# A two-layer decoder trunk on one core: one block of value products per group, two queues for the first loads, an earlier first norm

## The chip, the cores and the metric

The kernel runs on one core of one Trainium2 chip. The metric is the device time of one execution in microseconds (us); less is better. Five engines share the work: TensorE (PE in the profile, its weight loads are PEld), VectorE (DVE), ScalarE (ACT), GpSimd (POOL) and SyncE (SP), which here only issues transfers. Transfers are issued on the queues of SP, ACT and POOL and are carried by 16 DMA engines.

## The reference

Two pre-norm layers on x of 256 tokens by 2048 features, all float32, and a last norm. Layer 0 mixes by forgetting attention (32 heads of 64), layer 1 by sliding-window attention (32 query heads, 4 key and value heads, a learned sink per head, rotation of 16 of 64 dimensions).

```python
# layer 0
h = rmsnorm(x, norm_g[0]);  p = h @ fox_w_in          # q, k, v, gate: 2048 columns each, and 32 for f
log_f = log_sigmoid(p_f + b_f);  c = cumsum(log_f)
s = q k^T / 8 + c[t] - c[s], causal
y = softmax(s) @ v;  x = x + (y * silu(gate)) @ fox_w_out
# layer 1
h = rmsnorm(x, norm_g[1]);  p = h @ swa_w_in          # q, gate: 2048 columns each, k, v: 256 each
s = rope(q) rope(k)^T / 8, keys of the last 128 tokens
y = softmax with the sink in its sum @ v;  x = x + (y * silu(gate)) @ swa_w_out
# end
rmsnorm(x, final_g)
```

## The kernel before

**Weights as units and parts.** Every projection is cut into units of 256 output columns (`Unit`, L162). A unit is loaded in transfers of up to 1 MB on SP's queue (`load`, L187), split on chip into a rounded high half (a cast on ACT, L203) and a low rest (a subtraction on DVE, L204), and multiplied part by part (`block`, L206): for each of the 16 slices of 128 features a 512-column matmul (high weights on both halves of the activations) and a 256-column one. A part has 1 to 4 slices. A unit makes two accumulators (c = 0 and 1). The order on TensorE is: part i for c = 0, then part i-1 for c = 1. The very first value unit, 288 columns wide with the 32 columns of f, uses three 288-column matmuls per slice.

**Ticks.** Two slices of 512-column matmuls, or two of 256, make one tick (`tick`, L105), so a part of 4 slices is 4 ticks for each c. All attention work is hung into this stream by numbers: `after(n, fn)` (L102) lets `fn` write its instructions n ticks later. A scheduler then places what was written; TensorE's matmuls stay in the order written, other engines' instructions may move ahead where nothing holds them.

**Groups.** Layer 0 has 8 groups of 4 heads (two pairs each), and a group's units are q, k, gate, v. Layer 1 has k and v once, and then 8 groups of q, gate. For each pair (`Pair`, L341): `s` makes scores, softmax and the normalised weights `st`; `t` turns `st` of one head by three transposes into PSUM (`pt`, pool `ps_t`, one buffer) and copies it to `pts`; `pv` multiplies `pts` by the values into PSUM (`psy`, pool `ps_y`, one buffer), multiplies by the gate and splits the result into `ys`. `FOX_DUE`, `FOX_FIRST`, `FOX_LAST`, `SWA_DUE` and `SWA_LAST` (L39 to L43) give the ticks of s, t and pv for the two pairs of a group, counted from the end of that group's k (layer 0) or q (layer 1) for c = 0.

**The start.** Group 0's v, q and k are loaded in small parts (`V_PARTS`, `QK_PARTS`) between slices of x (`XP`, `XF`, L763). `split_x` makes the high and low half of a slice of x, `square_x` sums its squares. `NORM0` = 82 ticks after the start `norm0` (L784) sums the squares over features on TensorE (`ps_n`) and makes the factor r of the first norm. Until r is there, the first group's q, k and v are copied out of PSUM, and what needs r waits in a list (`when_normed`, L422). `FORGET` ticks after the values are scaled, `forget` (L391) transposes the f columns (`zt` into `pt_z`) and makes c; `FORGOT` = 20 ticks later c is transposed back (`pt_c`). The bias of a pair (`bc`) is read back from DRAM by GpSimd, which adds the causal mask `fmask` (L496). 9 matmuls on ones come first (`warm`, L117). The sinks of layer 1 are read at the start on GpSimd's queue (L839).

## Time and profile before

| | us |
|---|---|
| median of 3 runs | 858.47 (857.77 to 859.59) |
| profiled execution, its own time | 857.08 |
| span of that execution in the trace | 855.2 |
| TensorE busy in the span | 837.9 |
| VectorE busy | 665.6 |
| ScalarE busy | 547.9 |
| GpSimd busy | 88.1 |

The mean granted TensorE clock of the core is 0.992 of full speed. The profile's views used below are: the page's busy times and its chain of work that ended last; the waits (who waited for whom); the timeline (one row per run of like instructions: start in us, us to the end of the last, engine, line, operation, operands, count, and in brackets the idle time of the engine before and what ended it); the chain in order of time (start, us, what, count); and windows (for each stretch in us: its length, busy us and count for each engine, granted clock of TensorE, mean busy share of the DMA engines, GB/s).

### The profile page before, as it was taken

What the parts mean: (1) busy time and instruction counts of PE and PEld (TensorE: products, weight loads), DVE (VectorE), ACT (ScalarE), POOL (GpSimd) and SP (SyncE); (2) the same over time, 40 slices, a digit from 0 to 9 for tenths busy, and PEclk for the clock granted to TensorE, in tenths of its full rate; (3) what the DMA queues carried; (4) which work ended last, traced back from release to release, by engine and by line L of the source; (5) the groups of instructions that cost most, each with busy time, mean ns of one, the idle gap of its engine ahead of it and who ended that gap; (6) DMA issues with size and microseconds to landing.
All of it is one profiled execution on the core that took longest, in us unless ns stands there. A gap on an engine that the chain in (4) does not pass through costs nothing.

```text
span 855.2 us, 13619 instructions
## 1 busy us (share of the span) xinstructions
PE 837.9 (98%) x5038; PEld 726.0 (85%) x5038; DVE 665.6 (78%) x1410; ACT 547.9 (64%) x1080; POOL 88.1 (10%) x78
## 2 busy tenths in 40 slices
PE   8989999999999999999999999999999999999995
PEld 6968888888888888888888888888888888888885
DVE  6699968869686886868667778798898889976554
ACT  7576766747566674756655556577676776676562
POOL 1014100202011030300011110000000000003210
PEclk9989999999999999999999999999999999999998
DMA  7856455555555555554375555453544444355523
GB/s 241 282 175 229 167 176 187 191 190 187 184 181 173 190 189 188 191 177 144 128 254 186 176 185 193 155 189 108 190 149 148 148 149 156 140 178 180 191 99 98
DMA packets 28689, 150.51 MB, mean 176 GB/s; under 512 B 3232, under 2 KB 8256, under 8 KB 13008
## 3 DMA queue, kind: packets, MB, share of 16 engines
q1 hardware_dynamic: 25040, 142.09, 47.8%
q0 software_dynamic: 1408, 6.36, 2.5%
q10 hardware_dynamic: 2176, 1.20, 0.5%
q8 instruction: 39, 0.64, 0.3%
q14 instruction: 26, 0.21, 0.1%
HBM read 147.50 MB, written 2.15 MB: 175 GB/s over the span
## 4 chain that ended last, share of the span: by engine, by line
PE 90%; DVE 4%; DMA 3%; ACT 2%; issue 0%; SPq 0%; DVEq 0%; ACTq 0%
PE acc L73 81%; PE ps_s L73 3%; DMA wraw<-in_fox_in_dram 3%; PE psy L73 3%; PE pt L76 2%; DVE w L204 2%; ACT w L203 1%; ACT st L305 0%; DVE st L295 0%; SPq L198 0%; DVE xT L662 0%; DVE gt L276 0%; DVE kk L458 0%; DVE kk L457 0%; ACT xs L155 0%
## 5 line engine op out<-in xcount | busy, mean ns | idle before, releaser
L73 PE MATMUL acc<-xs,w 128*128 128x512 f32 (+1 forms) x2624 | 490.1, 341 | 1.7 <-ACT w L203 1.5
L73 PEld LDWEIGHTS acc<-xs,w 128*128 128x128 f32 x2624 | 408.0, 189 | 62.1 <-issue 4.8
L204 DVE TENSOR_TENSOR w<-wraw,w 128x1024 fp32r<-128x1024 f32 (+3 forms) x271 | 329.5, 1221 | 110.6 <-ACT w L203 108.6
L203 ACT CAST w<-wraw 128x1024 fp32r<-128x1024 f32 (+3 forms) x271 | 277.6, 1028 | 139.9 <-PE acc L73 124.1
L73 PE MATMUL acc<-ys,w 128*128 128x512 f32 x960 | 171.0, 338 | 0.0
L73 PEld LDWEIGHTS acc<-ys,w 128*128 128x128 f32 x960 | 147.5, 189 | 21.5 <-issue 0.5
L73 PE MATMUL acc<-w,xs 128*128 128x256 f32 (+2 forms) x608 | 114.0, 335 | 1.3 <-ACT w L203 0.8
L73 PEld LDWEIGHTS acc<-w,xs 128*128 128x128 f32 x608 | 92.3, 189 | 11.7 <-ACT w L203 1.1
L250 ACT COPY half<-acc 128x256 f32<-128x256 f32 x112 | 41.4, 370 | 46.2 <-PE acc L73 46.0
L305 ACT ACTIVATE st<-st,mx 128x128 f32<-128x128 f32 (+1 forms) x128 | 56.7, 444 | 8.8 <-DVE mx L508 8.1
L496 POOL TENSOR_TENSOR bc<-bc,fmask 128x768 f32<-128x768 f32 x16 | 42.6, 2664 | 49.7 <-DMA bc<-negc_d 46.7
L360 ACT COPY pts<-pt 128x384 f32<-128x384 f32 x64 | 30.4, 475 | 17.6 <-PE pt L76 17.6
L571 POOL TENSOR_TENSOR acc<-acc,sq 128x256 f32<-128x256 f32 x28 | 30.0, 1070 | 105.1 <-ACT sq L565 105.1
L569 POOL COPY acc<-sq 128x256 f32<-128x256 f32 x2 | 1.9, 936 | 337.1 <-ACT sq L565 337.1
L73 PE MATMUL ps_s<-kk,q 128*128 128x128 f32 (+1 forms) x256 | 35.5, 281 | 0.1
L316 DVE TENSOR_SCALAR st<-st,rl 128x128 f32<-128x128 f32 (+1 forms) x128 | 32.4, 316 | 0.8
L73 PEld LDWEIGHTS ps_s<-kk,q 128*128 128x128 f32 x256 | 32.2, 191 | 0.7 <-DVE kk L458 0.2
L76 PE MATMUL pt<-ident,st 128*128 128x128 f32 x192 | 31.8, 274 | 0.6 <-ACT pts L360 0.3
L495 POOL DMA_DIRECT2D bc<-negc_d x16 | 8.7, 547 | 205.5 <-DVE mx L507 146.5
L76 PEld LDWEIGHTS pt<-ident,st 128*128 128x128 f32 x192 | 23.5, 140 | 5.6 <-ACT pts L360 1.4
L156 DVE SCALAR_TENSOR_TENSOR xs<-xT,g_sb,xs 128x256 fp32r<-128x256 f32 x32 | 22.2, 716 | 2.9 <-ACT xs L155 2.9
L305 ACT ACTIVATION_READ_ACCUMULATOR st<-st,mx 128x1 f32 x128 | 23.9, 187 | 0.0
(136 smaller groups left out, 587.7 us busy)
## 6 DMA issues: line engine op xcount, KB each, us to landing
wraw<-in_fox_in_dram SPq DMA_DIRECT2D x58, 1024.0 KB, 4.9
wraw<-in_swa_in_dram SPq DMA_DIRECT2D x36, 1024.0 KB, 4.9
wraw<-in_fox_out_dram SPq DMA_DIRECT2D x14, 1024.0 KB, 4.8
wraw<-in_swa_out_dram SPq DMA_DIRECT2D x14, 1024.0 KB, 4.9
bc<-negc_d POOLq DMA_DIRECT2D x16, 384.0 KB, 3.8
wraw<-in_fox_in_dram SPq DMA_DIRECT2D x6, 512.0 KB, 5.6
wraw<-in_fox_out_dram SPq DMA_DIRECT2D x4, 512.0 KB, 3.6
wraw<-in_swa_out_dram SPq DMA_DIRECT2D x4, 512.0 KB, 3.5
```

The source lines that it names most:

```text
L73: tc.keep_in_program_order(nc.tensor.matmul(*args, **kw))
L76: tc.keep_in_program_order(nc.tensor.transpose(out, in_, ident))
L156: nc.vector.scalar_tensor_tensor(out=xs[:, kt, 1, :], in0=xT[:, kt, :], scalar=g, in1=xs[:, kt, 0, :].bitcast(F32), op0=ALU.mult, op1=ALU. ...
L203: state["split"] = nc.scalar.copy(w[:, :, 0, :], raw)
L204: nc.vector.tensor_tensor(out=w[:, :, 1, :], in0=raw, in1=w[:, :, 0, :].bitcast(F32), op=ALU.subtract)
L250: nc.scalar.copy(s, ps[:, S : 2 * S])
L305: nc.scalar.activation(st[:, hh, rng], st[:, hh, rng], AF.Exp, bias=nm[:, qb, hh : hh + 1], accum_out=l[:, qb, hh : hh + 1],)
L316: nc.vector.tensor_scalar_mul(st[:, hh, rng], st[:, hh, rng], rl[:, qb, hh : hh + 1])
L360: nc.scalar.copy(self.pts[hh], pt[:, 0 : 3 * P])
L495: nc.gpsimd.dma_start(out=bc, in_=negc_d[h0 : h0 + 2, :].partition_broadcast(P))
L496: nc.gpsimd.tensor_add(bc, bc, fmask.unsqueeze(1).to_broadcast([P, 2, 3 * P]))
L571: nc.gpsimd.tensor_add(sums[0], sums[0], s)
```

## The change

- **Value products.** `pv` of each pair is replaced by `Group.values`: both pairs of a group are multiplied in one block into one PSUM tile of 512 columns, at one due time per group. In layer 1, where both pairs of a group use the same values, one product covers both pairs (512 columns and 2x128 instead of twice 256 and 128). The gate product and the split into `ys` run on 512 columns at a time, in place in `gt`; for the last group of layer 1 (`singly`) they run pair by pair. `pts` of a group is one tile per head of the pair.
- **PSUM.** `ps_y` is gone; `ps_t` has two buffers, which transposes and `psy` share.
- **Start.** The first parts of v and q are read on ACT's queue, x entirely on SP's. x comes in 6 transfers of 1, 1, 2, 4, 4, 4 slices instead of 9, and v's last four parts in 2 transfers of 6 slices instead of 4 of 3. `PLAN` writes the order of loads, splits and squares out. 8 warm matmuls instead of 9.
- **First norm.** At tick 62 instead of 82, ahead of the end of the first units, so `when_normed` goes: v's results are scaled as they leave PSUM. `FORGET` is 8.
- **Due times** of the second pair's scores and transposes in layer 0 move by a few ticks.
- **Mask and sinks.** The causal mask is set into `bc` by two selects on its two diagonal blocks instead of an addition of `fmask`. The read of the sinks is written at step 300.

```diff
-WARM = 9
-V_PARTS = (1, 1, 2, 3, 3, 3, 3)
+WARM = 8
+V_PARTS = (1, 1, 2, (3, 3), (3, 3))
-NORM0 = 82
-FORGET = 6
+NORM0 = 62
+FORGET = 8
+SINK = 300
-FOX_DUE = ((16, 34, 80), (32, 58, 106))
-FOX_FIRST = ((46, 66, 90), (62, 82, 106))
-FOX_LAST = ((14, 32, 80), (34, 72, 86))
-SWA_DUE = ((16, 40, 52), (44, 64, 74))
-SWA_LAST = ((26, 45, 56), (30, 56, 68))
+FOX_DUE = ((16, 34), (40, 60), 106)
+FOX_FIRST = ((46, 68), (74, 94), 114)
+FOX_LAST = ((14, 32), (38, 72), 86)
+SWA_DUE = ((16, 40), (44, 64), 74)
+SWA_LAST = ((26, 45), (30, 56), 68)
...
-    ps_t = ctx.enter_context(tc.tile_pool(name="ps_t", bufs=1, space=bass.MemoryType.PSUM))
-    ps_y = ctx.enter_context(tc.tile_pool(name="ps_y", bufs=1, space=bass.MemoryType.PSUM))
+    ps_t = ctx.enter_context(tc.tile_pool(name="ps_t", bufs=2, space=bass.MemoryType.PSUM))
...
-    nc.scalar.dma_start(out=xT[:, 1:2, :], in_=xt_d[:, 1:2, :])
+    raw_v0 = work.tile([P, 6 * P], F32, tag="pts0", name="wraw", bufs=1)
+    nc.scalar.dma_start(out=raw_v0[:, 0 : 256 + H], in_=vf_d[:, 0, :])
+    raw_q0 = work.tile([P, S], F32, tag="row", name="wraw", bufs=4)
+    nc.scalar.dma_start(out=raw_q0, in_=fox_in_d[0, 0, 0][:, 0, :])
...
-        def pv(self):
-            psy = ps_y.tile([P, 512], F32, tag="Y", name="psy")
-            for hh in range(2):
-                o = psy[hh * HD : (hh + 1) * HD, :]
-                mm(o[:, 0:S], self.v_of(0, hh), self.pts[hh][:, 0:S], start=True, stop=False)
-                mm(o[:, P:S], self.v_of(1, hh), self.pts[hh][:, S : 3 * P], start=False, stop=True)
-            yt = work.tile([P, S], F32, tag="row", name="yt", bufs=4)
-            nc.vector.tensor_mul(yt, psy[:, 0:S], self.gate())
-            nc.scalar.copy(ys[:, self.kt, 0, :], yt)
-            nc.vector.tensor_sub(ys[:, self.kt, 1, :], yt, ys[:, self.kt, 0, :].bitcast(F32))
...
+        def values(self, kt, singly, shared):
+            psy = ps_t.tile([P, 512], F32, tag="T", name="psy")
+            for js in [slice(0, 2)] if shared else [slice(j, j + 1) for j in range(2)]:
+                for hh in range(2):
+                    o = psy[hh * HD : (hh + 1) * HD, :].rearrange("p (j n) -> p j n", j=2)[:, js, :]
+                    p = self.pts[hh][:, js, :]
+                    v = [self.v_of(js.start, b, hh) for b in range(2)]
+                    mm(o, v[0], p[:, :, 0:S], start=True, stop=False)
+                    mm(o[:, :, P:S], v[1], p[:, :, S : 3 * P], start=False, stop=True)
+            y = self.gt
+            for js in [slice(j, j + 1) for j in range(2)] if singly else [slice(0, 2)]:
+                out = ys[:, kt + js.start : kt + js.stop]
+                psj = psy.rearrange("p (j n) -> p j n", j=2)[:, js, :]
+                nc.vector.tensor_mul(y[:, js, :], psj, y[:, js, :])
+                nc.scalar.copy(out[:, :, 0, :], y[:, js, :])
+                nc.vector.tensor_sub(out[:, :, 1, :], y[:, js, :], out[:, :, 0, :].bitcast(F32))
...
-            nc.scalar.copy(vg, ps[:, 0:256])
-            nc.scalar.copy(zt, ps[:, 256 : 256 + H])
-            def rest():
-                r = r0()[:, S + c : S + c + 1]
-                nc.scalar.mul(zt, zt, r)
-                nc.scalar.mul(vg, vg, r)
-                if c == 1:
-                    after(FORGET, lambda: forget(state["zt"]))
-            when_normed(rest)
+            r = r0()[:, S + c : S + c + 1]
+            nc.scalar.mul(zt, ps[:, 256 : 256 + H], r)
+            nc.scalar.mul(vg, ps[:, 0:256], r)
+            if c == 1:
+                after(FORGET, lambda: forget(state["zt"]))
...
-                nc.gpsimd.tensor_add(bc, bc, fmask.unsqueeze(1).to_broadcast([P, 2, 3 * P]))
+                for hh in range(2):
+                    diagonal = bc[:, hh, :].rearrange("p (b k) -> p b k", k=P)[:, 0:3:2, :]
+                    fill_where_not(diagonal, [[0, 2], [-1, P]], 0, 1)
...
-    XP = [(0,), (1,), (2, 3), (4, 5), (6, 7), (8, 9), (10, 11), (12, 13), (14, 15)]
-    XF = [3, 6, 9, 9, 12, 13, 15, 16, 19]
+    XP = [(0, 1), (1, 2), (2, 4), (4, 8), (8, 12), (12, 16)]
+    PLAN = "x0 s0 w2 w3 x1 s1 w6 x2 s2 w9 x3 w10 s3 w11 q0 q1 x4 w12 x5 w13 q2 q3 s4 w14 q4 q5 s5 q6 q7 w15 w16"
...
-    nc.gpsimd.dma_start(out=sink, in_=sink_d.partition_broadcast(P))
+    after(SINK, lambda: nc.gpsimd.dma_start(out=sink, in_=sink_d.partition_broadcast(P)))
```

The program's rows at the places that the prediction speaks of follow. `acc` are the accumulators of the units, `xs` the split x, `w` a split part; 128x288 rows belong to the first value unit, 128x512 and 128x256 rows to q, k and, behind `pt_z`, the gate.

TensorE around the first norm, before:

```order
L73 MATMUL acc<-w,xs 128x288 x3
L73 MATMUL ps_n_504<-ssq_109,ones 128x256
L73 MATMUL ps_n_504<-ones,ssq_109 128x1 x2
L73 MATMUL acc<-w,xs 128x288 x6
L73 MATMUL acc<-xs,w 128x512 x4
L73 MATMUL acc<-xs,w 128x256 x4
L73 MATMUL acc<-xs,w 128x512 x4
L76 MATMUL pt_z<-ident,zt 32x128 x2
```

TensorE around the first norm, now (two more rows, of 4 matmuls with 512 and 4 with 256 columns, and then `pt_z` follow on the last row shown):

```order
L73 MATMUL ps_n_419<-ssq_108,ones 128x256
L73 MATMUL ps_n_419<-ones,ssq_108 128x1 x2
L73 MATMUL acc<-xs,w 128x256 x4
L73 MATMUL acc<-w,xs 128x288 x9
L73 MATMUL acc<-xs,w 128x512 x4
L73 MATMUL acc<-xs,w 128x256 x4
L73 MATMUL acc<-w,xs 128x288 x18
L73 MATMUL acc<-xs,w 128x512 x4
L73 MATMUL acc<-xs,w 128x256 x4
L73 MATMUL acc<-w,xs 128x288 x9
L73 MATMUL acc<-xs,w 128x512 x4
L73 MATMUL acc<-xs,w 128x256 x4
```

Between `ps_n` and `pt_z` TensorE had 18 matmuls; now it has 72. Ahead of `ps_n` stood 50 accumulating matmuls more than now, and `pt_z` stands 4 further back. ScalarE at the same place now (the casts of `w` with a DMA wait are those of the next parts to come, the one behind the two `r_n` rows is the gate's first):

```order
L210 CAST w<-wraw 128x4x256 [waits DMAHW7_49,DVE_49,PE_49]
L147 ACTIVATE r_n_425<-v_n_423 128x258 [waits DVE_49]
L148 ACTIVATE r_n_425<-r_n_425 128x258 [waits Activation_49]
L210 CAST w<-wraw 128x4x256 [waits DMAHW0_49,PE_49]
L482 ACTIVATE zt<-acc,r_n_425 128x32 [waits DVE_49,PE_49]
L483 ACTIVATE vg<-acc,r_n_425 128x256
L210 CAST w<-wraw 128x4x256 [waits PE_49]
L257 COPY half<-acc 128x256 [waits PE_49]
L482 ACTIVATE zt<-acc,r_n_425 128x32 [waits PE_49]
```

The scaled f columns (`zt`), which `pt_z` waits for, are now read from PSUM in one step each, and stand behind the casts of the gate's first two parts.

GpSimd at the start, before:

```order
L113 DMA bf_sb<-in_bf_dram 32x1
L389 MEMSET once 32x256
masks.py:197 MEMSET ident 128x128
L832 MEMSET fmask 128x384
masks.py:199 ISA
masks.py:199 AFFINE_SELECT ident<-ident 128x128 [waits Pool_49]
L122 AFFINE_SELECT fmask<-fmask 128x128 [waits Pool_49]
L122 AFFINE_SELECT fmask<-fmask 128x128
L839 DMA sink<-in_sink_dram 128x32
L836 COPY smask<-fmask 128x384 [waits Pool_49]
L122 AFFINE_SELECT smask<-smask 128x128 [waits Pool_49]
L404 DMA negc_d<-once 32x128 [waits DVE_49]
```

and now:

```order
L116 DMA bf_sb<-in_bf_dram 32x1
L407 MEMSET once 32x256
masks.py:197 MEMSET ident 128x128
L834 MEMSET smask 128x384
masks.py:199 ISA
masks.py:199 AFFINE_SELECT ident<-ident 128x128 [waits Pool_49]
L125 AFFINE_SELECT smask<-smask 128x128 [waits Pool_49]
L125 AFFINE_SELECT smask<-smask 128x128 x2
L839 DMA sink<-in_sink_dram 128x32
L422 DMA negc_d<-once 32x128 [waits DVE_49]
```

The read of the sinks, though written at step 300, stands where it stood: one select further back, ahead of the first row that waits for the forget gate, and with no wait of its own.

TensorE at the value products of layer 1, before (the four `psy` rows come twice per group) and now (once per group):

```order
L73 MATMUL acc<-xs,w 128x256 x4
L73 MATMUL psy<-pts,vs 64x256
L73 MATMUL psy<-pts,vs 64x128
L73 MATMUL psy<-pts,vs 64x256 [waits Activation_49]
L73 MATMUL psy<-pts,vs 64x128
L73 MATMUL acc<-xs,w 128x512 x4
```

```order
L73 MATMUL acc<-xs,w 128x512 x4
L73 MATMUL psy<-pts,vs 64x512 [waits Activation_49]
L73 MATMUL psy<-pts,vs 64x2x128
L73 MATMUL psy<-pts,vs 64x512 [waits Activation_49]
L73 MATMUL psy<-pts,vs 64x2x128
L73 MATMUL acc<-xs,w 128x256 x4
```

Eight products in two places have become four in one. In layer 0 the eight products stay eight, in one place.

More of the change, by code (lines that the diff above doesn't have):

```diff
@@ L190, in load @@
         if off == 0:
-            for tag, size, bufs in STAGES:
-                if unit.early and total * n <= size:
-                    raw = work.tile([P, size], F32, tag=tag, name="wraw", bufs=bufs)
-                    break
+            given = unit.stages[p] if p < len(unit.stages) else None
+            if given is None:
+                raw = wpool.tile([P, 2048], F32, tag="wraw", name="wraw", bufs=3)
+            elif isinstance(given, tuple):
+                tag, size, bufs = given
+                raw = work.tile([P, size], F32, tag=tag, name="wraw", bufs=bufs)
             else:
-                raw = wpool.tile([P, 2048], F32, tag="wraw", name="wraw", bufs=3)
+                raw = given
             raw = raw[:, 0 : total * n].rearrange("p (k n) -> p k n", n=n)
-            nc.sync.dma_start(out=raw, in_=src)
+            if given is None or isinstance(given, tuple):
+                nc.sync.dma_start(out=raw, in_=src)
             unit.raw = raw
@@ L202, in load @@
         w = w[:, 0 : 2 * s * n].rearrange("p (k h n) -> p k h n", h=2, n=n)
-        state["split"] = nc.scalar.copy(w[:, :, 0, :], raw)
+        nc.scalar.copy(w[:, :, 0, :], raw)
         nc.vector.tensor_tensor(
@@ L278, in consume @@
                 silu(group.gt[:, c : c + 1, :])
-                group.gates[c] = g
             elif c == 1:
                 silu(group.gt)
-                group.gates = [group.gt[:, j, :] for j in range(2)]
         return consume
@@ L341, in trunk, with __init__ @@
     class Pair:
-        def __init__(self, kt, scores, v_of, gate, prepare=None):
-            self.kt, self.scores, self.v_of, self.gate = kt, scores, v_of, gate
-            self.prepare = prepare
-            self.pts = [None, None]
+        def __init__(self, j, scores, prepare=None):
+            self.j, self.scores, self.prepare = j, scores, prepare
         def early(self):
@@ L376, in later, with attend @@
             after(s, self.s)
-            after(t, lambda: self.t(0))
-            after(t + 4, lambda: self.t(1))
-            after(pv, self.pv)
+            after(t, lambda: self.t(0, group))
+            after(t + 4, lambda: self.t(1, group))
+    class Group:
+        def attend(self, kt, due, singly, shared):
+            self.pts = [None, None]
+            for j, (s, t) in enumerate(due[0:2]):
+                self.pair(j).later(self, s, t)
+            after(due[2], lambda: self.values(kt, singly, shared))
+        def values(self, kt, singly, shared):
[14 more added lines that the diff above has]
+                nc.vector.tensor_sub(out[:, :, 1, :], y[:, js, :], out[:, :, 0, :].bitcast(F32))
     fox_scope = tc.tile_pool(name="fox", bufs=2)
@@ L460, in k_rest @@
             if c == 0:
-                p0, p1 = self.pair(0), self.pair(1)
-                for pair, d in zip((p0, p1), {0: FOX_FIRST, 7: FOX_LAST}.get(self.g, FOX_DUE)):
-                    pair.later(*d)
+                due = {0: FOX_FIRST, 7: FOX_LAST}.get(self.g, FOX_DUE)
+                self.attend(2 * self.g, due, False, False)
         def v(self, c, ps):
@@ L526, in trunk @@
         if g == 0:
[L527 removed]
+            row, gt, st = ("row", S, 4), ("gt", 2 * S, 3), ("st", 6 * P, 2)
+            uv = Unit(
+                cut(lambda a, b: vf_d[:, a:b], V_PARTS), "tok", G.v, n=256 + H, halves=False,
+                stages=(raw_v0, ("pts1", 6 * P, 1), st),
+            )
             uq, uk = (
@@ L530, in trunk @@
                     cut(lambda a, b, w=fox_in_d[i, 0]: w[a // 8][:, a % 8 : a % 8 + b - a], QK_PARTS),
-                    "wgt", consume, early=True, acc=acc,
+                    "wgt", consume, stages=(first, row, gt), acc=acc,
                 )
-                for i, consume, acc in ((0, G.q, None), (1, G.k, (ps_s, "S")))
+                for i, consume, first, acc in ((0, G.q, raw_q0, None), (1, G.k, row, (ps_s, "S")))
             )
@@ L722, in q @@
             if c == 0:
-                p0, p1 = self.pair(0), self.pair(1)
-                for pair, d in zip((p0, p1), SWA_LAST if self.u == 7 else SWA_DUE):
-                    pair.later(*d)
+                self.attend(2 * self.u, SWA_LAST if self.u == 7 else SWA_DUE, self.u == 7, True)
         def pair(self, j):
```

92 lines of the change are left out of this document (38 added, 54 removed).

## The prediction, made before the changed kernel ran

> **What bounds the kernel now.** I read the page's busy times and chain first, then windows over the whole span, then TensorE's waits, and then the stretch that these point to.
>
> ```profile
> PE 837.9 (98%) x5038; PEld 726.0 (85%) x5038; DVE 665.6 (78%) x1410; ACT 547.9 (64%) x1080; POOL 88.1 (10%) x78
> PE 90%; DVE 4%; DMA 3%; ACT 2%; issue 0%; SPq 0%; DVEq 0%; ACTq 0%
> ```
>
> TensorE is 90% of the chain that ended last. So time goes only by fewer or cheaper matmuls, or where TensorE stands still. Windows (length, busy, clock, DMA share, GB/s) show where that is:
>
> ```profile
> 40.00:45.00 5.00, 4.19 (x26) 3.44 (x24) 2.95 (x4) 2.57 (x5) 0.00 (x0) 1.00 0.84 336
> 45.00:50.00 5.00, 2.19 (x8) 1.82 (x9) 3.96 (x10) 3.93 (x12) 0.00 (x0) 0.66 0.62 218
> 100.00:500.00 400.00, 399.92 (x2382) 345.76 (x2381) 302.47 (x575) 252.09 (x475) 48.90 (x35) 1.00 0.53 184
> 500.00:800.00 300.00, 300.00 (x1834) 259.77 (x1833) 251.89 (x622) 202.33 (x427) 11.53 (x10) 1.00 0.47 162
> ```
>
> From 100 to 800 us TensorE never stops. Between 45 and 50 us it works for 2.19 us only, and its granted clock falls to 0.66. What it waited for (total, times, longest):
>
> ```profile
> PE pt_z L76 <- ACT zt L481: 3.5, 1, 3.5
> PE acc L73 <- ACT w L203: 2.3, 2, 1.5
> PE acc L73 <- DVE w L204: 0.7, 2, 0.4
> PE pt L76 <- ACT pts L360: 0.3, 1, 0.3
> ```
>
> Three sums can thus change: that one wait, the 3.0 us of first loads and splits, and the cost of matmuls. Waits for the copy of `pts` are 0.3 us in all, so a second transpose buffer is worth nothing by itself.
>
> **The first norm: the wait and the clock.** TensorE's timeline there, and then the other engines':
>
> ```profile
> 22.90 1.36 PE L73 MATMUL acc<-w,xs 128*128 128x288 f32 x9
> ...
> 30.47 2.95 PE L73 MATMUL acc<-xs,w 128*128 128x512 f32 x16
> 40.47 0.50 PE L73 MATMUL ps_n<-ones,ssq 128*128 128x1 f32 x4
> 41.70 2.49 PE L73 MATMUL acc<-xs,w 128*128 128x512 f32 x12
> 47.66 0.92 PE L76 MATMUL pt_z<-ident,zt 128*32 128x128 f32 x2 [3.47 <-ACT zt L481]
> 48.23 9.62 PE L73 MATMUL acc<-xs,w 128*128 128x256 f32 x40
> 57.79 0.31 PE L76 MATMUL pt_c<-ident,c 32*128 32x32 f32 x2
> ```
>
> ```profile
> 24.27 0.33 SPq L198 DMA_DIRECT2D wraw<-in_vf_dram  x1
> 29.12 0.92 ACT L203 CAST w<-wraw 128x864 fp32r<-128x864 f32 x1
> 33.74 0.41 DVE L782 TENSOR_TENSOR ssq<-ssq 128x256 f32<-128x256 f32 x1
> 40.96 1.05 ACT L203 CAST w<-wraw 128x1024 fp32r<-128x1024 f32 x1 [3.22 <-DMA wraw<-in_fox_in_dram]
> 42.05 2.36 DVE L204 TENSOR_TENSOR w<-wraw,w 128x1024 fp32r<-128x1024 f32 x2 [3.32 <-ACT w L203]
> 44.33 0.42 DVE L142 TENSOR_SCALAR v_n<-ps_n 128x258 f32<-128x258 f32 x1
> 47.83 0.30 ACT L481 ACTIVATE zt<-zt,r_n 128x32 f32<-128x32 f32 x1
> 54.09 0.67 DVE L402 TENSOR_TENSOR_SCAN c<-once 32x256 f32<-32x256 f32 x1
> ```
>
> `ps_n` is done at 40.97, but its reader on DVE starts at 44.33, behind two splits of the gate's weights; r and the scaled `zt` are there at 48. TensorE, out of work at 44.2, stands at `pt_z` for 3.47 us, its two transposes take 0.57 us until 48.23 (the later pair, `pt_c`, takes 0.31), and the next 40 matmuls take 9.62 us at the lowered clock. At full clock 40 such matmuls take 7.00 us (chain in order of time):
>
> ```profile
> 106.29 7.00 PE acc L73 x40
> 613.06 0.33 PE pt L76 x3
> 616.04 2.78 PE acc L73 x16
> 618.82 0.81 PE psy L73 x8
> 619.62 4.40 PE acc L73 x24
> 764.66 74.71 PE acc L73 x440
> ```
>
> So the late norm costs 3.47 + (0.57 - 0.31) + (9.62 - 7.00) = 6.35 us. The change puts `ps_n` 50 matmuls earlier and 72 ahead of `pt_z`. Of the 72, 36 are 288 columns wide (1.36 / 9 = 0.15 each) and 36 are of the kind that takes 7.00 / 40 = 0.175: 11.7 us of TensorE work. The chain from the end of `ps_n` to the scaled `zt` took 48.13 - 40.97 = 7.2 us with its two splits in front, so it fits with over 4 us to spare. What is late next, on ACT, is the gate's first cast, which now stands ahead of `zt`. If the gate lands at 40.96 as before, two casts (2.1), two `zt` (0.6), and a scaling of `vg` and a copy of about the copies' mean each
>
> ```profile
> L250 ACT COPY half<-acc 128x256 f32<-128x256 f32 x112 | 41.4, 370 | 46.2 <-PE acc L73 46.0
> ```
>
> end near 44.4, and TensorE wants `pt_z` at about 33 + 0.5 + 11.7 = 45. A wait of 0 to 1 us; I take 0.2.
>
> With `pt_z` early, the next link is its chain to `pt_c`, 40 matmuls later: it took from 47.66 to 54.76, 7.1 us, and was hidden since those matmuls ran for 9.62. At full clock they give 7.0 plus the transposes' 0.3. I take 0.2 (0 to 1).
>
> The moved `ps_n` gets a wait of its own: behind it the whole of TensorE's queue stands until the squares are summed. TensorE reaches its new place near 33 us (30.47 plus 12 of the 16 matmuls, 2.3, plus the 0.4 of the next part). The sum of squares was ready at 34.15. x now comes in front of most weights, but the last addition stands on DVE behind the first split of v's last transfer (864 KB), and that is issued when DVE has done the transfer before it, at about 24.5 (worked out in the next part). Before, half as much, issued at 24.27, was cast at 29.12, 4.85 us later; the other 432 KB at the 336 GB/s of the window from 40 us add 1.3. So a cast at 30.6 and, with 0.92, a split of 1.06 and the addition of 0.41, the sum at 33.0, against TensorE's 33. I take a wait of 0.3, bounds 0 and 1.5.
>
> **The first loads.**
>
> ```profile
> 1.06 4.21 PE L73 MATMUL warm<-ones 128*128 128x128 f32 x18 [1.06 <-DVE ones L115]
> ...
> 9.90 0.85 PE L73 MATMUL acc<-xs,w 128*128 128x512 f32 x2 [1.47 <-ACT w L203]
> ```
>
> ```profile
> 3.50 0.57 POOL L839 DMA_DIRECT2D sink<-in_sink_dram  x1
> 13.57 1.71 ACT L155 ACTIVATE xs<-xT,g_sb 128x256 fp32r<-128x256 f32 x4
> 15.18 1.14 ACT L779 ACTIVATE sq<-xT 128x512 f32<-128x512 f32 x2
> 17.55 1.93 ACT L203 CAST w<-wraw 128x1024 fp32r<-128x1024 f32 x2 [0.28 <-DMA wraw<-in_fox_in_dram]
> 22.24 0.92 ACT L203 CAST w<-wraw 128x864 fp32r<-128x864 f32 x1 [0.63 <-DMA wraw<-in_vf_dram]
> 23.19 1.06 DVE L204 TENSOR_TENSOR w<-wraw,w 128x864 fp32r<-128x864 f32 x1
> ```
>
> Two loads move from SP's queue to ACT's and one from ACT's to SP's: SP's queue is ahead by one issue net (0.33 us at 24.27), up to two with what stands between. That shortens the early waits (1.47 at 9.90, 3.0 in all) by so much at most. But v's fourth part, which TensorE took up at 22.90 without waiting, moves back on ACT: behind k's cast (17.55 to 18.6) now stand four splits of x (1.71) and two squares (1.14), then its own cast of 0.92 ends at 22.4 and its low half on DVE (1.06) at 23.4. The second matmul of that part needs the low half, so TensorE goes on 0.4 us later than before, whatever it won earlier. Its second half is then split by 24.5. Bounds: 0.7 us won (two issues), 1.3 lost (twice the bytes, the 432 KB of above, if v's landing and not ACT decides); I take a loss of 0.3. The sinks change nothing: their read stands in the same place, one select later.
>
> **The value products.** In the chain, 16 + 24 accumulating matmuls with a block of value products between them take 2.78 + 0.81 + 4.40 = 7.99 us, and 40 without one 7.00: a block costs 0.99 us. Its columns are two passes over 256 and 128, so six of 128, and a transpose of 128 columns takes 0.33 / 3 = 0.11: 0.66 us. The other 0.33 us is paid on entering and leaving. A group has two blocks and will have one: 1.98 becomes 1.32 + 0.33 = 1.65, a gain of 0.33 us in each of 16 groups, 5.3 us. Bounds: 0.81 - 0.66 = 0.15 per group, 2.4 us, if only what lies inside the block's own row goes; 0.45, 7.2 us, if the halved number of products in layer 1 saves something besides. I take 0.33: it is the measured difference, and 0.15 would need the rest to be paid at some other place of the same chain. [...]
>
> **Costed at nothing.** On ACT and DVE the gate products and splits get wider and fewer; TensorE waits for neither from 100 to 800 us, and behind the last group of layer 1 it ran 440 matmuls without a stop from 764.66. There the later pair's results come one set of three operations later, some 1.2 us; cover are the 16 ticks (32 matmuls at 0.175, 5.6 us) from the products to the part that reads them. Without cover that is 1.2 us once. The masks on GpSimd get cheaper, off the path. The moved due times keep 20 ticks from scores to transposes, where first pairs do with 18. One warm matmul less: 0.
>
> **Sum.** 6.35 - 0.2 - 0.2 - 0.3 - 0.3 + 5.3 = 10.65 us off the profiled execution's own 857.08 gives 846.4; that execution lies 1.39 under the median of 858.47, so 847.8 as a median. Own range, with the bounds: 844.5 to 851.
>
> **Rivals.**
> - *The norm's wait only moves.* If the sum of squares or the gate's landing is late by over 3 us, TensorE idles and the clock falls again. For: both stand behind a transfer of 864 or 1024 KB. Against: the estimates leave at most 1.5. Then only the products pay: 858.47 - 5.3 + 0.3 = 853.5. Chance 0.11.
> - *Blocks cost by products, not by blocks.* The entry price comes back between the two pairs: 2.4 us or less instead of 5.3, 850.7. For: the second pair of layer 0 loads new weights. Against: a block's passes follow one another at column speed. Chance 0.09.
> - *The clock starts late.* 18 passes of 9 warm matmuls kept TensorE busy from 1.06 to 5.27 at 0.23 us each; with 8 it stops 0.47 us sooner. If the full clock then comes only after the first wait, the matmuls from 5.27 to 8.43 (the wait of 1.47 ends at 9.90) take twice their time at worst, 3.2 us more, of which the wait hides 1.47: +1.7, 849.5. For: the clock did fall after 3.47 us without work. Against: the gap is a seventh of that. Chance 0.06. [...]
> - *The sinks do move.* If their read leaves the start in spite of the rows, the wait of 1.47 goes with it: 846.3. Chance 0.03.
> - *Slower.* `ps_n` at tick 62 stops TensorE until the squares are there. An idle time d costs d and, as above, 2.6 us of clock; it loses against before from d = 10.65 + 0.3 - 2.6 = 8.3 us, the sum ready after 41 us. It was ready at 34.15 with x last in line, now x is earlier. At d = 9.5: 859.7. Chance 0.03.
>
> **How the numbers follow.** The forecast has 0.68. The range of 8 in 10 takes in the second, third and fourth rival and half of the first: 844.5 to 852.5. A measurement tells about 0.2% (1.7 us) from no change; all cases but the last are faster by more: faster 0.95, same 0.02, slower 0.03.
>
> **What would show it.** Right: no wait at `pt_z` over 1 us, a granted clock of 1.00 from 45 to 55 us, `ps_n` between 32 and 35 us, 16 groups of `psy` rows of about 1.5 us, the last wait of TensorE before 35 us, the read of the sinks issued before 5 us. Wrong: a clock under 1 after the first 10 us, a wait for `ssq`, or `psy` with its neighbours at 1.8 us or more per group.

## The result, and the profile after

The changed kernel takes 844.65 us as the median of 4 runs (844.48 to 844.79), the kernel before 858.84 us beside it (857.77 to 859.59). The ratio is 0.9836, 95% interval 0.9819 to 0.9853. The profiled execution took 844.48 us with a span of 842.7 us, so 12.6 us less than the profiled execution of before, where the forecast had 10.65; the forecast median was 847.8.

The page's line of busy times, and the one of the chain of waits:

```profile
PE 830.0 (98%) x4972; PEld 720.9 (86%) x4972; DVE 656.7 (78%) x1380; ACT 542.6 (64%) x1061; POOL 67.8 (8%) x93
PE 94%; DVE 4%; ACT 1%; issue 1%; DMA 0%; ACTq 0%; DVEq 0%
```

TensorE's share of the chain went from 90 to 94%, and GpSimd's busy time from 88.1 to 67.8 us. The second looked like nothing on the page; it was not. The windows around the place of the old stall (length, busy time of each engine, clock, DMA share, GB/s), and all that TensorE waited for in the first 80 us:

```profile
40.00:45.00 5.00, 5.00 (x34) 4.59 (x33) 3.57 (x5) 3.68 (x10) 0.00 (x0) 1.00 0.85 316
45.00:50.00 5.00, 5.00 (x30) 4.33 (x30) 4.80 (x14) 4.80 (x11) 0.20 (x1) 1.00 0.13 54
50.00:55.00 5.00, 5.00 (x30) 4.31 (x30) 4.96 (x9) 2.62 (x5) 1.91 (x4) 1.00 0.32 74
```

```profile
PE acc L73 <- DVE w L211: 1.4, 3, 0.9
PE acc L73 <- ACT w L210: 1.1, 2, 0.8
PE warm L73 <- DVE ones L118: 1.1, 1, 1.1
```

TensorE works without a stop from 40 to 55 us and the granted clock stays at 1.00, where before it worked 2.19 of 5 us and the clock was at 0.66. What waits are left lie in the first 23 us, as TensorE's timeline shows, and at the kernel's tail, where both kernels stand for 2.55 us ahead of the last `rows` product:

```profile
5.13 1.03 PE L73 MATMUL acc<-w,xs 128*128 128x288 f32 x3 [0.37 <-ACT w L210]
...
11.29 0.40 PE L73 MATMUL acc<-w,xs 128*128 128x288 f32 x1 [0.75 <-ACT w L210]
12.09 0.92 PE L73 MATMUL acc<-w,xs 128*128 128x288 f32 x5 [0.39 <-DVE w L211]
...
22.73 1.33 PE L73 MATMUL acc<-w,xs 128*128 128x288 f32 x8 [0.88 <-DVE w L211]
...
32.61 0.59 PE L73 MATMUL ps_n<-ssq,ones 128*128 128x256 f32 x2
...
44.36 0.38 PE L76 MATMUL pt_z<-ident,zt 128*32 128x128 f32 x2
44.49 7.26 PE L73 MATMUL acc<-xs,w 128*128 128x512 f32 x40
```

The wait of 1.47 us at 9.90 is gone; a new one of 0.88 us stands at v's fourth part; `ps_n` at 32.61 and `pt_z` at 44.36 wait for nothing, and the 40 matmuls behind `pt_z` take 7.26 us in place of 9.62.

**Where the time went.** Both kernels issue the same 4,288 accumulating matmuls, so one can read when each starts the n-th of them (n from 0, in us of the span):

| n | 80 | 90 | 200 | 320 | 500 | 2300 | 4287 |
|---|---|---|---|---|---|---|---|
| before | 22.90 | 24.33 | 41.70 | 70.75 | 110.33 | 459.66 | 845.50 |
| changed | 21.55 | 24.14 | 41.56 | 64.15 | 102.37 | 449.63 | 833.22 |
| lead | 1.35 | 0.19 | 0.14 | 6.60 | 7.96 | 10.03 | 12.28 |

Up to 200 lie the first loads: 1.35 us won, and all but 0.19 given back at v's fourth part. From 200 to 320 lies the first norm: 6.46 us. From 320 to 500 lies the first group's attention, with its block of value products: 1.36 us. From there to 2300 lie the other seven groups of layer 0: 2.07 us, 0.30 each. Behind that lie the eight groups of layer 1: 2.25 us, 0.28 each. Of the 12.5 us between the spans, 0.2 fall behind the last matmul.

### The profile page after: what moved, and what is told of

Its sections match the earlier page's. It is cut to its first block, busy times and chain, and to the rows that moved or that the text cites. A ratio compares the mean times of both kernels' runs of the same rounds, so it can differ in the third digit from the quotient of the medians.

```text
span 842.7 us, 13456 instructions
## 1 busy us (share of the span) xinstructions
PE 830.0 (98%) x4972; PEld 720.9 (86%) x4972; DVE 656.7 (78%) x1380; ACT 542.6 (64%) x1061; POOL 67.8 (8%) x93
## 3 DMA queue, kind: packets, MB, share of 16 engines
q10 hardware_dynamic: 2320, 1.35, 0.5%
## 4 chain that ended last, share of the span: by engine, by line
PE 94%; DVE 4%; ACT 1%; issue 1%; DMA 0%; ACTq 0%; DVEq 0%
PE acc L73 85%; PE ps_s L73 3%; PE psy L73 3%; PE pt L76 2%; DVE w L211 1%; ACT w L210 1%; DMA wraw<-in_vf_dram 0%; DVE st L299 0%; DVE xs L159 0%; DVE xT L667 0%; DVE ssq L784 0%; ACT st L309 0%; DVE q L330 0%; PE ps_n L73 0%; DVE st L320 0%
## 5 line engine op out<-in xcount | busy, mean ns | idle before, releaser
L73 PE MATMUL acc<-xs,w 128*128 128x512 f32 (+1 forms) x2624 | 483.2, 339 | 0.2 <-DVE w L211 0.2
L211 DVE TENSOR_TENSOR w<-wraw,w 128x1024 fp32r<-128x1024 f32 (+3 forms) x271 | 325.1, 1204 | 108.1 <-ACT w L210 106.1
L125 POOL TENSOR_SCALAR_AFFINE_SELECT bc<-bc 128x256 f32<-128x256 f32 x32 | 22.9, 737 | 56.7 <-DMA bc<-negc_d 56.7
L329 ACT CAST q<-qT 64x256 fp32r<-64x256 f32 x32 | 12.8, 401 | 18.6 <-DVE qT L697 18.2
```

What stands on the lines that cost most here:

```text
L73: tc.keep_in_program_order(nc.tensor.matmul(*args, **kw))
L125: nc.gpsimd.affine_select(out=ap, in_=ap, compare_op=ALU.is_ge, fill=NEG, base=base, pattern=pattern, channel_multiplier=mult,)
L211: nc.vector.tensor_tensor(out=w[:, :, 1, :], in0=raw, in1=w[:, :, 0, :].bitcast(F32), op=ALU.subtract)
L329: nc.scalar.copy(q2[w, hh, :], t[w, :])
```

## The experiments

At the 90th matmul, executions whose first 20 us are the same program lie up to 1.2 us apart, and a lead won or lost there stays to the end. So differences under 1 us are read from the lead as in the table above, taken behind the 200th matmul, and not from the medians alone.

**1. The norm's tick alone.** In the kernel before:

```diff
-NORM0 = 82
+NORM0 = 62
```

> The kernel before with one number changed: the norm's tick 62 in place of 82. Theory (the late norm cost a stall and a lowered clock, and nothing else of the change is needed to win it back): the wait of 3.5 us at pt_z is gone, the clock is 1.00 from 45 to 55 us, which takes 6.5 us off; x is still last in line, so ps_n waits about 1 us for its squares (ready at 34.15, TensorE there near 33). Profiled 857.1 - 6.5 + 1.1 = 851.7. If the lowered clock is also what made the timed runs of before longer than the profiled one and unlike each other, the timed runs here lie within 0.4 us of each other. Rival (the gain at the norm needs the earlier x and the longer transfers): the wait at pt_z stays over 2 us or comes back at ps_n, 855 to 858, runs spread over 1 to 2 us as before.

855.61 us (854.38 to 859.16), ratio 0.9973 (0.9957 to 0.9989); profiled 855.47 in place of 857.08. The tick alone brings 1.6 us between the profiled executions, and 2.3 by the ratio of all runs. What TensorE waited for:

```profile
PE acc L73 <- ACT w L203: 2.5, 2, 1.6
PE pt_z L76 <- ACT zt L481: 2.0, 1, 2.0
...
PE ps_n L73 <- DVE ssq L782: 1.0, 1, 1.0
```

The wait for the squares came as expected (0.98), the one at `pt_z` did not go. ScalarE's timeline tells why:

```profile
45.08 0.19 ACT L477 COPY zt<-acc 128x32 f32<-128x32 f32 x1
45.16 1.06 ACT L203 CAST w<-wraw 128x1024 fp32r<-128x1024 f32 x1
46.74 0.83 ACT L325 CAST q<-q 64x256 fp32r<-64x256 f32 x2 [0.52 <-DVE q L440]
47.59 0.32 ACT L481 ACTIVATE zt<-zt,r_n 128x32 f32<-128x32 f32 x1
```

r was there at 41, but between the second copy of `zt` and its scaling stand a weight's cast and two casts of q, which themselves wait for VectorE. The rival's time is the nearer one, and its reason holds for `ps_n`; the wait at `pt_z` has another. The runs still differ among themselves by 4.8 us: that a lowered clock alone makes the spread of before is not shown by this run.

**2. The tick with the short consumer.** The same, and the consumer of v and forget as the change has it:

```diff
-NORM0 = 82
-FORGET = 6
+NORM0 = 62
+FORGET = 8
...
-            nc.scalar.copy(vg, ps[:, 0:256])
-            nc.scalar.copy(zt, ps[:, 256 : 256 + H])
...
+            nc.scalar.mul(zt, ps[:, 256 : 256 + H], r)
+            nc.scalar.mul(vg, ps[:, 0:256], r)
```

> The kernel before with the norm at tick 62, and with what the change does to the consumer of v and the forget gate: the two scalings read the sums in PSUM directly, zt first, without a copy ahead, and the transposes come 8 ticks behind it in place of 6. Theory (in the run with tick 62 alone pt_z waited 2.0 us for its second zt, which stood on ACT behind a copy, a cast of a weight and two casts of q; the earlier norm is worth its 6.5 us only with the consumer shortened): no wait over 0.3 us at pt_z, the wait of 1 us at ps_n stays, profiled 853.6 - 2.0 - 0.3 for the waiting transpose = 851.3. Rival (ACT's place behind the gate's first loads decides, and those arrive 4 us later here than in the changed kernel): the wait at pt_z stays over 1 us, 852.5 to 853.6.

(The expected sum starts from the span of the run before it, 853.6, and not from its time, 855.47; it should read 853.2.) Measured 855.9 us (853.93 to 857.67), ratio 0.9974 (0.9961 to 0.9986). The trace is of the slowest of its 12 runs. Nothing waits at `pt_z` any more, as the theory said. But the wait moved to `ps_n`; TensorE's timeline, and two windows:

```profile
35.04 0.70 PE L73 MATMUL ps_n<-ssq,ones 128*128 128x256 f32 x2 [2.00 <-DVE ssq L776]
...
37.01 2.36 PE L73 MATMUL acc<-w,xs 128*128 128x288 f32 x9
```

```profile
36.00:37.00 1.00, 1.00 (x5) 1.00 (x6) 1.00 (x2) 0.00 (x0) 0.00 (x0) 0.50 0.59 221
38.00:39.00 1.00, 1.00 (x6) 1.00 (x6) 0.68 (x1) 0.97 (x3) 0.00 (x0) 0.50 0.92 303
```

With x last in line the squares are summed at 35, and behind a stop of 2.00 us the granted clock reads 0.50 in both windows (from 35.9 to 39.3 us, an estimate from windows of 1 and 2 us): nine matmuls that take 1.36 us at full clock take 2.36. Up to the 320th matmul this kernel leads before by 2.56 us, the changed one by 6.60. Against before it then loses 1.8 us at the first group's transposes, and 1.4 us in later groups of layer 0, where three waits of transposes for the copy of `pts` name 0.7 of it. So both theory and rival miss: the third part that the norm needs is the early x.

**3. The early x without the tick.** In the changed kernel tick 82, forget 6 ticks later, and the consumers of v, q and k storing and scaling later, as before:

```diff
-NORM0 = 62
-FORGET = 8
+NORM0 = 82
+FORGET = 6
...
+    def when_normed(fn):
+        if "r0" in state:
+            fn()
+        else:
+            state["after_norm"].append(fn)
```

> The changed kernel with only the norm put back: tick 82, the consumers of v, q and k storing their sums and scaling them once r is there, forget 6 ticks later, as before. x stays early. Theory (the 6.5 us come from the tick, the early x and the shorter consumer together, and x alone wins nothing): TensorE stands at pt_z for 2.5 to 3.5 us and the clock falls behind it, 844.65 + 3.0 + 0.3 + 2.6 = 850.5 (849.5 to 851.5). Rival (the gate's first loads, which now land 3 to 4 us earlier, had held up the norm's chain on DVE and ACT; then the tick decides little): a wait under 1.5 us and no lowered clock, 844.7 to 846.

849.16 us (847.51 to 849.84), 4.5 us above the changed kernel; in the lead, 4.6 us between the 200th and the 320th matmul. TensorE's timeline and a window:

```profile
46.63 0.30 PE L76 MATMUL pt_z<-ident,zt 128*32 128x128 f32 x1 [2.65 <-ACT zt L498]
47.15 0.40 PE L76 MATMUL pt_z<-ident,zt 128*32 128x128 f32 x1 [0.22 <-ACT zt L498]
47.20 8.59 PE L73 MATMUL acc<-xs,w 128*128 128x256 f32 x40
```

```profile
47.00:48.00 1.00, 0.85 (x5) 0.85 (x6) 0.54 (x2) 0.97 (x4) 0.00 (x0) 0.50 0.00 0
```

The stall and the lowered clock come back, as the theory said, 1.3 us below its number and just under its range: the clock is low for 3.4 us here and was for 6.8 us before. Taken together: early x with the late norm leaves 4.6 of the 6.46 us unwon, and the early norm with the late x leaves 3.8 (from the 90th to the 320th matmul it wins 2.64 us, the changed kernel 6.41). Neither stands for the gain by itself. Here tick and consumer are put back together; a version with only the longer consumer wasn't run.

**4. Two blocks of value products again.** In the changed kernel:

```diff
-            after(due[2], lambda: self.values(kt, singly, shared))
+            for j, pv in enumerate(due[2]):
+                after(pv, lambda j=j: self.values(kt, j))
...
-FOX_DUE = ((16, 34), (40, 60), 106)
+FOX_DUE = ((16, 34), (40, 60), (80, 106))
...
-SWA_DUE = ((16, 40), (44, 64), 74)
+SWA_DUE = ((16, 40), (44, 64), (52, 74))
```

> The changed kernel with the value products of each group in two blocks again, the first pair's 22 to 26 ticks (FOX_LAST: 6, SWA_LAST: 12) ahead of the second's, eight products per pair in both layers. Theory (what costs is entering and leaving a block): 0.29 us for each of 16 groups, 844.65 + 4.6 = 849.3 (848.7 to 850). Rival (it is the number of products): only layer 1 has more products, 8 groups of 0.28: 846.9. Rival (neither; the gain came from the PSUM buffers or the due times): 844.6 to 845.

849.54 us (849.47 to 849.57): 4.89 above the changed kernel, inside the theory's range. In the lead it is 4.73 behind the 200th matmul, 0.296 per group. The chain in order of time, of this run and of the changed kernel (one block of layer 0, one of layer 1):

```profile
113.89 0.81 PE psy L73 x8
124.25 0.81 PE psy L73 x8
```

```profile
88.03 1.50 PE psy L73 x16
562.26 1.45 PE psy L73 x8
```

Two blocks hold 1.62 us of the chain, the one of layer 0 holds 1.50 and that of layer 1 1.45: 0.12 or 0.17 us of the 0.296 are won inside the rows, the rest on the way in and out.

**5. Sixteen products in layer 1's block in place of eight.**

```diff
-self.attend(2 * self.u, ..., self.u == 7, True)
+self.attend(2 * self.u, ..., self.u == 7, False)
```

> The changed kernel with sixteen products in layer 1's block in place of eight, still one block. Theory (entering and leaving decides): at most the 0.05 us by which layer 0's block of sixteen (1.50 us) is longer than layer 1's of eight (1.45 us), eight times: 844.7 to 845.1. Rival (the number of products decides): the whole 0.28 us per group of layer 1 comes back, 846.9.

845.34 us (845.11 to 845.69). In layer 1 the lead falls by 0.41 us, 0.05 per group, and its blocks measure as layer 0's do:

```profile
671.47 1.50 PE psy L73 x16
```

So the number of products is worth 0.4 us in all. Experiment 4 had the sixteen products too, so the number of blocks is worth the rest of its 4.7: 4.3 us, 0.27 per group. The theory's mechanism holds, though the median lies 0.24 us over its range; the traced execution had lost 0.17 us by the 200th matmul already.

**6. PSUM apart, and the first group's old due times.** Three runs ask where the first group's 1.07 us (1.36 less the 0.29 of its block) came from. First one transpose buffer and one value buffer:

```diff
-    ps_t = ctx.enter_context(tc.tile_pool(name="ps_t", bufs=2, ...))
+    ps_t = ctx.enter_context(tc.tile_pool(name="ps_t", bufs=1, ...))
+    ps_y = ctx.enter_context(tc.tile_pool(name="ps_y", bufs=1, ...))
...
-            psy = ps_t.tile([P, 512], F32, tag="T", name="psy")
+            psy = ps_y.tile([P, 512], F32, tag="Y", name="psy")
```

> The changed kernel with one transpose buffer and one value buffer in PSUM, as before, in place of two that both share. Theory of the prediction (a second transpose buffer is worth nothing by itself): no wait at pt over 0.1 us in the steady part, 844.5 to 844.9. Rival (the waits of the first group, 0.28 and 0.32 us by name and 1.07 us in all, went because of the second buffer): they come back, 845.7, with a wait at pt for the copy pts between 65 and 85 us.

845.11 us (844.78 to 845.71), a little over the theory's range and short of the rival's number. The lead falls by 0.26 us over the seven later groups of layer 0 and by nothing in the first, and no wait at `pt` shows by name. Then the due times alone:

```diff
-FOX_FIRST = ((46, 68), (74, 94), 114)
+FOX_FIRST = ((46, 66), (62, 82), 106)
```

> The changed kernel with the first group's due times of before: scores at 46 and 62, transposes at 66 and 82, products at 106. Theory (the waits of the first group went because of the later due times, not because of the second buffer, which was worth 0.0 there when it was taken away): two waits at pt come back between 70 and 85 us, 0.5 to 1.1 us in all, 845.2 to 845.8. Rival (they went with the earlier norm chain, which now lets the scores' inputs be ready): no waits, 844.5 to 844.8.

845.12 us (844.26 to 845.71); behind the 200th matmul the lead does not change by more than 0.1 us, and nothing waits at the transposes. Then both together:

> The changed kernel with both of the undone things that left the first group without waits when undone alone: one transpose buffer and one value buffer, and the first group's scores at 46 and 62 and transposes at 66 and 82. Theory (either of the two is enough, and before had neither): waits at pt of 0.5 to 1.1 us come back between 70 and 85 us, 845.3 to 845.9. Rival (neither had to do with it; ACT and DVE reach the scores earlier because the norm is early): no waits there, 844.7 to 845.2, the 0.26 us of the single buffer alone.

845.14 us (844.49 to 845.91). Again there is no wait in the first group, and the groups behind it lose 0.3 us of lead. The theory that either of the two was needed falls. The rival's reason, the early norm, isn't needed either: experiment 3 has the late norm, and its first group wins 1.38 us over before all the same.

**7. The masks.** What was left in that stretch is GpSimd. Of the kernel before, GpSimd's and VectorE's timelines there:

```profile
63.19 5.12 POOL L496 TENSOR_TENSOR bc<-bc,fmask 128x768 f32<-128x768 f32 x2 [2.80 <-DMA bc<-negc_d]
```

```profile
63.74 0.42 DVE L275 TENSOR_TENSOR gt<-acc,half 128x256 f32<-128x256 f32 x1
64.09 2.51 DVE L204 TENSOR_TENSOR w<-wraw,w 128x1024 fp32r<-128x1024 f32 x1
66.53 2.06 DVE L276 TENSOR_TENSOR gt<-gt,r_n 128x256 f32<-128x256 f32 x1
...
68.96 0.42 DVE L276 TENSOR_TENSOR gt<-gt,r_n 128x256 f32<-128x256 f32 x1
```

While GpSimd adds the mask, a product that takes VectorE 0.42 us takes 2.06, and a split that takes 1.22 takes 2.51. Both stretched rows lie on before's chain of work that ended last (in order of time):

```profile
64.16 2.45 DVE w L204
66.60 1.99 DVE gt L276
```

The changed kernel's chain holds nothing but TensorE's rows from 55 to 100 us. In the last of the runs of 6 the selects stand there instead, on GpSimd and VectorE:

```profile
60.36 2.47 POOL L126 TENSOR_SCALAR_AFFINE_SELECT bc<-bc 128x256 f32<-128x256 f32 x4 [5.51 <-DMA bc<-negc_d]
```

```profile
61.04 0.62 DVE L283 TENSOR_TENSOR gt<-gt,r_n 128x256 f32<-128x256 f32 x1
```

So the addition was put back into that kernel (its mask tile `fmask` is set up at the start again, not shown here):

```diff
-                for hh in range(2):
-                    diagonal = bc[:, hh, :].rearrange("p (b k) -> p b k", k=P)[:, 0:3:2, :]
-                    fill_where_not(diagonal, [[0, 2], [-1, P]], 0, 1)
+                nc.gpsimd.tensor_add(bc, bc, fmask.unsqueeze(1).to_broadcast([P, 2, 3 * P]))
```

> The kernel of the run before (apart PSUM buffers, the first group's old due times) with the masks of the first layer added to the bias on GpSimd as before (one TENSOR_TENSOR of 128x768 per pair), in place of two selects per pair. Theory (in the kernel before, GpSimd's addition ran 5.12 us for two beside VectorE, whose products of gt took 2.06 us there in place of 0.42 and whose split 2.51 in place of 1.22; that made the first group's scores late and gave TensorE its waits of 1.07 us in all): VectorE's rows between 59 and 80 us stretch to 2 us again, waits at pt between 68 and 85 us of 0.5 to 1.1 us in all, 845.14 + 0.8 = 845.9 (845.6 to 846.4). Rival (the stretched rows come back but the earlier norm leaves them room): the rows stretch, no wait at pt over 0.2 us there, 845.0 to 845.3. Rival (the rows stretch for another reason): no row of VectorE over 1.6 us there.

849.93 us (849.18 to 850.58): 4.8 us slower than without, far beyond the theory's own range. VectorE's timeline, TensorE's, and TensorE's waits:

```profile
61.02 2.07 DVE L283 TENSOR_TENSOR gt<-gt,r_n 128x256 f32<-128x256 f32 x1
63.01 0.41 DVE L282 TENSOR_TENSOR gt<-acc,half 128x256 f32<-128x256 f32 x1
63.46 1.62 DVE L283 TENSOR_TENSOR gt<-gt,r_n 128x256 f32<-128x256 f32 x1
```

```profile
70.78 0.61 PE L76 MATMUL pt<-ident,st 128*128 128x128 f32 x3 [0.64 <-DVE st L321]
...
77.81 0.61 PE L76 MATMUL pt<-ident,st 128*128 128x128 f32 x3 [0.49 <-ACT q L330]
...
80.13 0.55 PE L76 MATMUL pt<-ident,st 128*128 128x128 f32 x3 [0.30 <-ACT pts L364]
```

```profile
PE pt L76 <- ACT pts L364: 1.5, 7, 0.4
```

The first group loses 2.2 us, at the two waits that before has there (for q and for the copy `pts`) and one more for `st`. Experiments 1 and 2, with the same addition and the early norm, lose there too: 1.0 and 1.8 us against before. Each later group of layer 0 loses 0.35; waits for the copy out of the only transpose buffer name 1.2 of these 2.5 us. With one buffer and the first group's old due times, the selects are thus worth 4.7 us. That is not their gain over before, which has the addition and one buffer too and no wait at `pt` in its later groups; why not, no run shows. What the selects are worth with two buffers and the new due times wasn't tried.

**8. The first loads.** The sinks' read made to wait for the first norm, by a copy into their tile:

```diff
-    after(SINK, lambda: nc.gpsimd.dma_start(out=sink, ...))
+    def read_sink():
+        nc.gpsimd.tensor_copy(sink, state["r08"][:, 0:H])
+        nc.gpsimd.dma_start(out=sink, ...)
+    after(SINK, read_sink)
```

> The changed kernel with the read of the sinks made to wait for the first norm's result (a copy of a part of it into the sinks' tile stands ahead on GpSimd), so that it leaves the first 30 us. Theory of the prediction's rival (the read's slow packets hold up the first loads): the loads that were issued at 3.7 and 4.1 us and landed at 8.8 and 9.7 land 1 us or more earlier, and the wait of 0.75 us near 11 us goes: 843.6 to 844.2. Rival (the waits are set by bytes, or given back at v's fourth part, where TensorE stands for 0.88 us anyway): 844.4 to 844.8.

844.68 us (844.51 to 845.27), so no difference in time. Windows of one microsecond, of the changed kernel and of this run:

```profile
6.00:7.00 1.00, 1.00 (x8) 0.73 (x6) 0.72 (x3) 0.89 (x3) 0.00 (x0) 1.00 1.22 47
7.00:8.00 1.00, 1.00 (x7) 0.78 (x6) 1.00 (x3) 1.00 (x3) 0.00 (x0) 1.00 0.46 100
```

```profile
6.00:7.00 1.00, 0.86 (x4) 0.59 (x5) 0.42 (x1) 0.12 (x2) 0.00 (x0) 1.00 0.96 275
7.00:8.00 1.00, 0.95 (x5) 0.45 (x5) 0.60 (x2) 1.00 (x3) 0.00 (x0) 1.00 0.99 346
```

The read does hold up the loads (47 and 100 GB/s with it, 275 and 346 without). In each of the nine traces with the change's first loads and the early read, the slowest microsecond between 6 and 9 us has 47 to 180 GB/s; in the two without the read it has 275 and 280. The wait of 0.75 us is gone, and the trace leads the changed kernel's by 0.5 us. That is within what the starts differ by between executions. Then v's first 864 KB ahead of x's fifth transfer:

```diff
-"... q0 q1 x4 w12 x5 w13 q2 ..."
+"... q0 q1 w12 x4 x5 w13 q2 ..."
```

> The changed kernel with v's first 864 KB issued one transfer earlier, ahead of x's fifth, and so cast on ACT and split on DVE ahead of x's fifth splits and squares. Theory (TensorE's 1.15 us at v's fourth part, at 21.6 us, are ACT's and DVE's order): the wait there falls under 0.2 us, 843.5 to 844.0. Rival (it moves to the part that needs x's fifth transfer or to ps_n): 844.4 to 845.

843.73 us (842.92 to 843.81), and v's fourth part waits for nothing, as TensorE's timeline shows:

```profile
22.00 1.36 PE L73 MATMUL acc<-w,xs 128*128 128x288 f32 x9
```

This is 0.9 us faster than the changed kernel, inside the theory's range. Both edits together:

> The changed kernel with both edits at the start: v's 864 KB ahead of x's fifth transfer, and the sinks read behind the first norm. Theory (the two waits, 1.15 us at v's fourth part and 0.5 us of early ones, are set by different things): 844.65 - 0.9 - 0.5 = 843.2 (842.8 to 843.6). Rival (the early 0.5 us is lost again at a later wait, as TensorE only comes sooner to the same load): 843.6 to 844.0.

843.18 us (842.73 to 843.57), ratio to before 0.9812 (0.9796 to 0.9827), the theory's value, and 1.5 us under the changed kernel with no overlap of the runs. It is the fastest of the versions run. The 0.55 us between it and v's earlier load alone is not shown: the two versions' runs overlap, and the late read alone brought nothing.

## Why the prediction was right, step by step

Direction and size were right. The range, 844.5 to 851, held by 0.15 us at its low end, and it is narrower than its own bounds: added up, they give 844.2 to 854.5. That it held is partly luck, since 0.7 us too much for the value products set off part of what was missed elsewhere. The six signs named for it came: no wait at `pt_z`, the clock at 1.00 from 45 to 55 us, `ps_n` at 32.61, blocks of 1.50 and 1.45 us, the last wait ahead of the kernel's tail at 22.73, and the sinks' read still issued in the first 5 us, by GpSimd's timeline:

```profile
3.76 0.57 POOL L839 DMA_DIRECT2D sink<-in_sink_dram  x1
```

Of the signs of being wrong, a clock under 1 came in the tail alone (0.50 from 838 to 842 us), where before has it too (0.50 from 849 to 855).

The steps, in us off the profiled execution:

| Step | Forecast | Found |
|---|---|---|
| norm: wait, slow transposes, lowered clock | 6.35 | 6.46 |
| new waits at `pt_z` and `pt_c` | -0.4 | 0 |
| `ps_n` waits for the squares | -0.3 | 0 |
| first loads | -0.3 | 0.14 |
| value products | 5.3 | 4.6 |
| masks on GpSimd | 0 | 1.07 with the rest of that stretch |
| behind the last matmul and outside the span | 0 | 0.3 |
| sum | 10.65 | 12.6 |

- **The norm.** Size right, and for the reason given: the stall, and the clock behind it, are gone (1.00 from 40 to 55 us), and they come back when the norm is put back (experiment 3). What the prediction priced at 0.3 us as a side condition, the early sum of squares, is what the 6.46 us hang on: with x in its old place the stop moves to `ps_n` (1.0 and 2.0 us in experiments 1 and 2). The rival "the norm's wait only moves" is therefore a true mechanism which the order of x's transfers keeps away. VectorE's and ScalarE's timelines of the changed kernel have the last addition of the squares and the casts of v's second half:

```profile
30.19 0.43 DVE L786 TENSOR_TENSOR ssq<-ssq 128x256 f32<-128x256 f32 x1
```

```profile
28.26 1.74 ACT L210 CAST w<-wraw 128x864 fp32r<-128x864 f32 x2 [1.73 <-DMA wraw<-in_vf_dram]
```

The squares were summed 2.4 us earlier than worked out, at 30.6, since that half was cast at 28.26 and not at 30.6.
- **The first loads.** That v's fourth part would stand on ScalarE behind x's splits and squares, and that TensorE would then go on no earlier than before, is what happened: wait 0.88, lead 1.35 before it and 0.19 behind. The step that failed is the bound of 0.7 us on what could be won ahead of it. In the traced execution the new front of the queues won 1.35 us, with the wait of 1.47 us gone, and not two issues' worth. The sinks' read stayed where it was, at 3.76, and so did the slow microseconds of the loads behind it (47 GB/s from 6 to 7 us, 275 without the read, experiment 8).
- **The value products.** Mechanism right, by experiments 4 and 5: blocks decide (0.27 us each), products hardly (0.05). The term was mis-sized by 0.04 us per group, 0.7 in all: the block's streaming was put at 0.66 us from a transpose's 0.11 per 128 columns, and the rows give 1.50 - 0.81 = 0.69. Against 5.3 by the prediction's working and 2.4 by its lower bound, 4.6 to 4.7 was measured, so more goes with a block than what lies inside its row. What makes entering and leaving a block cost time, no run shows.
- **"The masks on GpSimd get cheaper, off the path."** This is the step that was wrong. GpSimd's time is off the path, but its additions slowed VectorE, which was not far enough off it: `gt<-gt,r_n` took 2.07 us beside an addition and 0.62 beside selects (experiment 7). In the two stretches shown there `gt<-gt,r_n` and `w<-wraw,w`, with both inputs in SBUF, are the rows that are stretched (2.06 us in place of 0.42, 2.51 in place of 1.22); `gt<-acc,half`, with one input in PSUM, takes 0.41 us between two of them. Not every such row is: in the kernel before, the split at 76.17 took 1.22 us beside the addition from 75.88, and there the addition took 3.22 us, where the shortest of the sixteen took 1.84. What the two engines share is not shown. The prediction put the first group's wait of 0.3 us for `pts` down to the transpose buffer, left out the other of 0.3 us for q, and gave that stretch no gain. That the whole 1.07 us is the masks' is argued from before's chain and from experiments 3, 6 and 7; no run changes the masks alone in the kernel before. That a second transpose buffer is worth nothing by itself held in the first group only: without it the later ones lose 0.26 us.
- **"The clock starts late."** This rival's condition did not come in the changed kernel's traced execution, where four 128x512 matmuls took 0.87 us from 6.94 on. Its sign, matmuls at about half pace, came most plainly in three others with the same 8 warm matmuls (experiment 6, first and last, and experiment 7). The last of 6 has, on TensorE's timeline:

```profile
8.08 1.48 PE L73 MATMUL acc<-xs,w 128*128 128x512 f32 x4
```

Two of the three are 1.2 us behind the changed kernel at the 90th matmul, the third is level with it. In the last of 6, three 128x288 matmuls from 7.36 us took 0.92 us (0.56 in the changed kernel, from 6.54), though the granted clock reads 1.00 there from 6 to 8 us, as it does in experiment 7. So part of what the starts differ by may be the pace of the matmuls and not the loads; that it is the clock was not shown, and no run separates the two, or shows whether a ninth warm matmul avoids it.
- **From the profiled execution to the median.** The prediction carried the 1.39 us by which the median of before lay above its profiled execution over to the changed kernel. There it was 0.17. So 1.2 of the 3.15 us between 847.8 and 844.65 are this offset, and 1.95 the sum.

## What to carry to other kernels

A wait is removed only when all that feeds its replacement is early too: the norm's gain came with the tick, the order of x's loads and a shorter consumer together, and the three versions with one or two of these left out lost 3.4 to 4.6 of some 6.4 us. An engine off the path with 8 to 10% of busy time can still set the end if the work of an engine near the path takes longer beside it; look for one form of instruction whose single durations differ by a factor (0.42 and 2.06 us), and for what ran beside it. What is paid per block of small matmuls between large ones was worth more (4.3 us) than the number of matmuls in it (0.4 us).
